# A hybrid transformer block on one core: a builder that plans every engine's order, and more seven-product quads

## The chip, the cores and the metric

The kernel runs on one core of one Trainium2 chip. The core has a matrix engine (TensorE, PE in the profile), a vector engine (VectorE, DVE), a scalar engine (ScalarE, ACT), a general engine (GpSimd, POOL) and a queue engine that issues most transfers (SyncE, SP). The metric is the device time of one execution in microseconds, the median of the runs; lower is better.

## The reference

One block of a language model, in 32-bit floats, for 256 tokens of width 2048. It is a feed-forward network, a mixer and a second feed-forward network, each between a norm before and a norm after, each added to the residual:

```python
def _swiglu(x, w_gate, w_up, w_down):                 # 2048 -> 5632 -> 2048
    return (jax.nn.silu(x @ w_gate) * (x @ w_up)) @ w_down

def _hybrid_mixer(u, ...):
    p = u @ w_in                                      # 2048 -> 3360 + 1024 + 2 * 2048
    z_a, z_b, g_a, g_b = jnp.split(p, IN_SPLITS, axis=-1)
    y_a = _rwkv7_branch(z_a, ...) @ w_proj_a          # 16 heads of 64, a recurrence over tokens
    y_b = _pool_branch(z_b, ...) @ w_proj_b           # windowed means, 4 groups
    m = jax.nn.sigmoid(g_a) * y_a + jax.nn.sigmoid(g_b) * y_b
    return m @ w_out

h = x + 0.5 * norm(_swiglu(norm(x), ffn1...))
h = h + norm(_hybrid_mixer(norm(h), ...))
out = h + 0.5 * norm(_swiglu(norm(h), ffn2...))
```

Nearly all the arithmetic is in the large products: the three weights of each feed-forward network, and `w_in`, `w_proj_a`, `w_proj_b`, `w_out` of the mixer.

## The kernel before

**A product.** A 32-bit product is made of three faster ones. Every operand is split into a high part (rounded to the fast format) and a low part (the rest): ACT writes the high part of a weight tile, `wH` (L149), DVE subtracts it from the tile and writes the low part, `wL` (L150), and `mm3` (L173 to L175) issues high x high, high x low and low x high into one PSUM bank. Tokens are the rows of the output: the activations, transposed, are the stationary operand (128 x 128), and 512 columns of a weight are the moving one. So one product of a weight row block k with one half h of the tokens is three matmuls of 128x512.

**Weights.** They come from DRAM as tiles of 128 x 1024 (two row blocks of 512 columns, 512 KB), issued by SP into four raw buffers `w32` (`get_w`, L135). Five buffers each of `wH` and `wL` follow. SP issues in order and waits for a free raw buffer.

**Quads.** Where two row blocks k, k+1, two column blocks (called f and l) and two token halves meet, eight products are needed. `seven` makes them with seven: it forms sums and differences of the weight tiles (`t13` at L344, `t24` at L349 and L350), splits them (L356 on ACT, L357 on DVE), multiplies them with sums of the activation tiles that were prepared once (`sums`), and puts the results together with adds on DVE from PSUM (`merge` at L381, `finish` at L391). One such step is called a quad here. `FAST = range(2, 10)` makes two quads in each of the eight inner blocks of gate and up, `NQ = 6` makes six in each of the two column pairs of the down product: 16 + 12 for each feed-forward network.

**A feed-forward network.** Gate and up are walked in 11 blocks of 512 columns. For a block, the f columns are those of the gate weight, the l columns those of the up weight. Then ACT makes a sigmoid and DVE multiplies (L613, L615), DVE multiplies with up (L619), and DVE turns the block in 32 x 32 squares (L545). For the down product the block's hidden units must lie on the partitions, so 16 ACT copies of 32 x 256 (L571, in `carry_at`) move the squares to the right partitions, one block later, and ACT and DVE split the result. The down product has 44 row blocks and two column pairs of 2 x 512 columns; `post` squares and sums its results for the norm, scales them and adds the residual.

**The mixer.** The products of `w_in` and of the projections fill TensorE while two halves of the heads (hf 0 and 1) go through the recurrence in chunks of 64 tokens: small matmuls (64 x 64), masks, and DVE and ACT work between them (`rwkv`). Two powers of -1/2 are made on GpSimd: the norm of the keys (L1162, 128 x 16) and the group norm of each chunk (L1386, 128 x 4).

**What sets the order.** Instructions go to each engine in program order. Large parts are ordered by hand: in the feed-forward networks, `put` gives PE work with its expected time, `at` places the ACT and DVE work at a moment of that clock, and `run` writes them out in time order; in the mixer, generators hand over PE time step by step (`weave`). Elsewhere a scheduler with priorities orders the instructions. Buffers rotate in pools.

Of the kernel before, what the change touches and what calls it, by code (L numbers as in the profile page):

```python
# [5 lines left out]

# [12 lines left out]
P = 128  # L19
# [8 lines left out]
C = 64  # L28
# [6 lines left out]
W32_BUFS = 4  # L35
WS_BUFS = 5
BOOST = 2000
MM, MC = 0.2265, 0.12
TT = 0.45
# [3 lines left out]
AHEAD = (5.0, 6.0)  # L43
TURNS = [[4.2, 5.3, 6.4, 7.5], [5.3, 6.0, 6.7, 7.4]]
WARM = 12
TB = 4
NQ = 6
QUADS = {False: ((7, 11, 15), (3, 6, 9)), True: ((2, 5, 8, 11, 14), (1,))}
FAST = range(2, 10)
# [5 lines left out]

class Block:
    def __init__(s, tc, ctx):
        s.tc = tc
        s.nc = nc = tc.nc
        E = ctx.enter_context  # L60
        s.n = 0
        s.late, s.after, s.items, s.events, s.now = [], [], deque(), [], 0.0
        s.clk, s.uses = 0.0, []
        s.cp = E(tc.tile_pool(name="cp", bufs=1))
        s.wp = E(tc.tile_pool(name="wp", bufs=3))
        s.up = E(tc.tile_pool(name="up", bufs=NUNITS))
        s.tp = E(tc.tile_pool(name="tp", bufs=TB))
        s.sp = E(tc.tile_pool(name="sp", bufs=4))
        s.dp = E(tc.tile_pool(name="dp", bufs=1, space=bass.MemoryType.DRAM))
        s.pm = E(tc.tile_pool(name="pm", bufs=4, space=PSUM))  # L70
        s.pt = E(tc.tile_pool(name="pt", bufs=4, space=PSUM))
        s.ident = s.const([P, P], "ident")
        make_identity(nc, s.ident)
        s.mhalf = s.const([P, 16], "mhalf")
        nc.gpsimd.memset(s.mhalf, -0.5)
# [4 lines left out]

    def const(s, shape, name, dt=F32):
        return s.cp.tile(list(shape), dt, tag=name, name=name)

    def unit(s, shape=(P, 1024), dt=F32, p="u"):
        return s.up.tile(list(shape), dt, tag="u", name=s.nm(p))

    def tmp(s, p="t"):
        return s.tp.tile([P, 512], F32, tag="t", name=s.nm(p))

    def rtmp(s, p="r"):  # L90
        return s.tp.tile([P, 256], F32, tag="r", name=s.nm(p), bufs=3)

    def small(s, w, tag, bufs=4):
        return s.sp.tile([P, w], F32, tag=tag, name=s.nm(tag), bufs=bufs)

    def psum(s, p="pt"):
        return s.pt.tile([P, 512], F32, tag="pt", name=s.nm(p))

    def at(s, t, fn):

        s.n += 1
        heapq.heappush(s.events, (t, s.n, fn))

    def slot(s, end):

        s.uses.append(end)
        n = len(s.uses) - 1 - WS_BUFS
        return s.uses[n] if n >= 0 else n - 1.0

    def run(s):  # L110

        s.now = 0.0
        E = mybir.EngineType
        with s.tc.manual_schedule(engines={E.PE, E.Activation, E.DVE}):
            while s.items or s.events:
                while s.events and (s.events[0][0] <= s.now or not s.items):
                    heapq.heappop(s.events)[2]()
                if s.items:
                    t, fn = s.items.popleft()
                    fn()  # L120
                    s.now += t
            s.stats()
        s.now = s.clk = 0.0
        s.uses = []

    def put(s, t, fn):
        s.items.append((t, fn))
        s.clk += t

    def get_w(s, w, j, n, c0, cw, own=False):  # L130
        if own:
            w32 = s.unit(p="w32")
        else:
            w32 = s.wp.tile([P, 1024], F32, tag="w32", name=s.nm("w32"), bufs=W32_BUFS)
        s.nc.sync.dma_start(out=w32[:, :n * cw].rearrange("p (k c) -> p k c", k=n),  # L135
                            in_=w[j * P:(j + n) * P, c0:c0 + cw]
                            .rearrange("(k p) c -> p k c", p=P))
        return w32

    def two(s, w32, j, n, cw, hold=False):  # L140
        if hold:
            wH, wL = s.unit(dt=F32R, p="kH"), s.unit(dt=F32R, p="kL")
        else:
            wH = s.wp.tile([P, 1024], F32R, tag="wH", name=s.nm("wH"), bufs=WS_BUFS)
            wL = s.wp.tile([P, 1024], F32R, tag="wL", name=s.nm("wL"), bufs=WS_BUFS)
        v, vH, vL = [t[:, :n * cw].rearrange("p (k c) -> p k c", k=n)
                     for t in (w32, wH, wL)]
        with s.tc.high_priority(offset=BOOST):
            s.nc.scalar.copy(vH, v)  # L149
            s.nc.vector.tensor_tensor(out=vL, in0=v, in1=vH.bitcast(F32), op=ALU.subtract)  # L150
        return [(j + i, vH[:, i], vL[:, i]) for i in range(n)]

# [8 lines left out]
    def split_w(s, fill):  # L161

        w32 = s.wp.tile([P, 1024], F32, tag="w32", name=s.nm("w32"), bufs=W32_BUFS)
        wH = s.wp.tile([P, 1024], F32R, tag="wH", name=s.nm("wH"), bufs=WS_BUFS)
        wL = s.wp.tile([P, 1024], F32R, tag="wL", name=s.nm("wL"), bufs=WS_BUFS)
        fill(w32.rearrange("p (a b) -> p a b", a=2))
        s.nc.scalar.copy(wH, w32)
        s.nc.vector.tensor_tensor(out=wL, in0=w32, in1=wH.bitcast(F32), op=ALU.subtract)
        return [t.rearrange("p (a b) -> p a b", a=2) for t in (wH, wL)]

    def mm3(s, ps, aH, aL, bH, bL, start, stop):
        nc = s.nc
        nc.tensor.matmul(ps, aH, bH, start=start, stop=False)  # L173
        nc.tensor.matmul(ps, aH, bL, start=False, stop=False)  # L174
        nc.tensor.matmul(ps, aL, bH, start=False, stop=stop)  # L175

    def gemm_tok(s, w, c0, at, KT, evac, lead=False, trail=False, xs=None, hold=False):
        pss = [s.pm.tile([P, 512], F32, tag="mm", name=s.nm("mm")) for _ in range(2)]
# [10 lines left out]
        def both(k0, k1):  # L189
            for k2 in range(k0, k1, 4):  # L190
                keep(s.load_w(w, k2, min(4, k1 - k2), c0, 512))
                for k in range(k2, min(k2 + 4, k1)):
# [3 lines left out]
        if trail:  # L196
            both(0, KT - TRAIL)
            s.by_half(w, c0, KT - TRAIL, KT, s.clk, AHEAD[0], do, keep,
                      lambda h: evac(h, pss[h]))
# [5 lines left out]
        elif lead:  # L205
            s.by_half(w, c0, 0, STAG, s.clk, AHEAD[1], do, keep)
            s.run()
            k0 = STAG
        both(k0, KT)
        if hold:  # L210
            for h in range(2):
                s.at(0.3 + 1.6 * h, lambda h=h: evac(h, pss[h]))
            return
        with s.tc.high_priority(offset=BOOST):
            for h in range(2):
                evac(h, pss[h])

    def gemm_at(s, w, c0, at, KT, evac):

        pss = []  # L220
        ws = {}

        def load(k):
            ws.update((i, (wH, wL)) for i, wH, wL in s.load_w(w, k, 2, c0, 512))

        def do(k):
            if not pss:
                pss.extend(s.pm.tile([P, 512], F32, tag="mm", name=s.nm("mm"))
                           for _ in range(2))
            for h in range(2):  # L230
                (wH, wL), (xH, xL) = ws[k], at(k)
                s.mm3(pss[h], xH[:, h * P:h * P + P], xL[:, h * P:h * P + P], wH, wL,
                      k == 0, k == KT - 1)
        for k in range(0, KT, 2):
            s.at(s.slot(s.clk + 12 * MM), lambda k=k: load(k))
            s.put(6 * MM, lambda k=k: do(k))
            s.put(6 * MM, lambda k=k: do(k + 1))
        for h in range(2):
            s.at(s.clk + 0.3 + 1.6 * h, lambda h=h: evac(h, pss[h]))

    def by_half(s, w, c0, k0, k1, start, ahead, do, keep, done=None):

        for k in range(k0, k1, 2):
            s.at(start + (k - k0) * 3 * MM - ahead,
                 lambda k=k: keep(s.load_w(w, k, 2, c0, 512, k - k0 >= STAG)))
        for h in range(2):
            for k in range(k0, k1):
                s.put(3 * MM, lambda k=k, h=h: do(k, h))
            if done:
                s.put(0, lambda h=h: done(h))  # L250

    def sums(s, T, out, when=None):
# [3 lines left out]
        tt = {}  # L256
        fl = lambda t: t.rearrange("p a b t -> p (a b t)")

        def first():
            xH, xL = T[len(out) // 2]  # L260
            x = tt["x"] = s.unit((P, 2, 2, S), F32, "sx")
            V.tensor_tensor(out=fl(x), in0=xH.bitcast(F32).rearrange("p k t -> p (k t)"),
                            in1=xL.bitcast(F32).rearrange("p k t -> p (k t)"), op=ALU.add)

        def second():
            x = tt["x"]
            a11, a21 = x[:, :, 0, :P], x[:, :, 0, P:]
            a12, a22 = x[:, :, 1, :P], x[:, :, 1, P:]
            f = tt["f"] = s.unit((P, 4, 2, P), F32, "sf")
            V.scalar_tensor_tensor(out=f[:, 0], in0=a21, scalar=-1.0, in1=a22, op0=ALU.mult,  # L270
                                   op1=ALU.subtract)
            V.scalar_tensor_tensor(out=f[:, 1], in0=f[:, 0], scalar=-1.0, in1=a11,
                                   op0=ALU.mult, op1=ALU.subtract)
            V.tensor_tensor(out=f[:, 2], in0=a11, in1=a21, op=ALU.subtract)
# [1244 lines left out]
```

## Time and profile before

| what | value |
|---|---|
| median of 3 runs | 2062.89 us (2062.83 to 2062.97) |
| profiled execution, span from first to last instruction | 2061.1 us |
| mean granted TensorE clock | 0.998 of full speed |
| PE / DVE / ACT / POOL busy | 2047.8 / 1638.5 / 1228.9 / 76.0 us |
| read from DRAM | 396.69 MB, 197 GB/s over the span |

The profiled execution was timed by its span alone; it lies 1.8 us below the median of the runs. A profile row names the line, the engine, the operation, `out<-in` by the tiles' names, shapes, how often it ran, busy time and the mean of one in ns, and what ended the idle time before it. `PE` is matmul, `PEld` the weight load that runs beside it. Successive matmuls overlap, so the length of one (about 0.39 us) is more than its share of the time.

### The profile page before, as it was taken

The numbers are of one execution on the slowest core, as the hardware profiler recorded it, in microseconds if no ns is written. First come the engines' busy times: TensorE is split into PE (matmuls) and PEld (weight loads), VectorE is DVE, ScalarE is ACT, GpSimd is POOL, SyncE is SP. The second block draws the span as 40 slices with busy tenths as digits, with TensorE's granted clock in tenths as the row PEclk, the third lists the DMA queues.
The fourth block names the chain that finished last, engine by engine and source line by source line (L and its number), as shares of the span: only waits on it lengthen the run. The fifth ranks groups of instructions, "written<-read, shape, count | busy, mean of one in ns | idle before, by whom it ended". The sixth has DMA issues, their size and how long they took to land.

```text
span 2061.1 us, 29467 instructions
## 1 busy us (share of the span) xinstructions
PE 2047.8 (99%) x10925; PEld 1726.6 (84%) x10925; DVE 1638.5 (79%) x2104; ACT 1228.9 (60%) x1752; POOL 76.0 (4%) x161
## 2 busy tenths in 40 slices
PE   9999999999999999999999999999999999999998
PEld 7888888888888899999888788888888888888886
DVE  6888889878787765799688666578888898787875
ACT  7667666766555574474465444466677667755553
POOL 0000000000000100000110110010000000000000
PEclk9999999999999999999999999999999999999999
DMA  7566666665667666656456565665666666656674
GB/s 259 174 195 210 195 205 194 199 220 173 215 205 254 218 188 185 179 161 199 129 158 190 163 245 187 202 215 173 194 207 195 212 194 195 220 167 218 208 251 151
DMA packets 225913, 407.02 MB, mean 197 GB/s; under 512 B 14943, under 2 KB 50921, under 8 KB 225769
## 3 DMA queue, kind: packets, MB, share of 16 engines
q1 hardware_dynamic: 219593, 384.69, 59.8%
q0 software_dynamic: 5888, 19.93, 2.7%
q8 instruction: 85, 1.39, 0.3%
q10 hardware_dynamic: 288, 0.52, 0.1%
q14 instruction: 59, 0.48, 0.1%
HBM read 396.69 MB, written 8.39 MB: 197 GB/s over the span
## 4 chain that ended last, share of the span: by engine, by line
PE 97%; issue 1%; DVE 1%; POOL 0%; DMA 0%; ACT 0%; POOLq 0%; DVEq 0%; SPq 0%; ACTq 0%
PE mm L173 26%; PE mm L175 25%; PE mm L174 25%; PE mc L500 10%; PE ms L173 2%; PE ms L175 2%; PE ms L174 2%; PE tr L528 1%; PE pA L1240 0%; PE pSa L1348 0%; PE pU L1336 0%; DMA w<-in_ffn_gate_dram 0%; DVE wL L150 0%; PE pT L1407 0%; PE pM L1306 0%
## 5 line engine op out<-in xcount | busy, mean ns | idle before, releaser
L150 DVE TENSOR_TENSOR wL<-w,wH 128x1024 fp32r<-128x1024 f32 (+2 forms) x613 | 730.3, 1207 | 274.7 <-ACT wH L149 271.2
L149 ACT CAST wH<-w 128x1024 fp32r<-128x1024 f32 (+2 forms) x613 | 631.0, 1043 | 425.9 <-PE mm L175 236.8
L173 PE MATMUL mm<-wH,xH 128*128 128x512 f32 x2124 | 830.2, 392 | 0.0
L175 PE MATMUL mm<-wH,xL 128*128 128x512 f32 x2124 | 827.2, 389 | 0.7 <-DVE xL L536 0.7
L174 PE MATMUL mm<-wL,xH 128*128 128x512 f32 x2124 | 826.9, 389 | 0.0
L175 PEld LDWEIGHTS mm<-wH,xL 128*128 128x128 f32 x2124 | 398.7, 188 | 84.8 <-DVE xL L536 1.5
L173 PEld LDWEIGHTS mm<-wH,xH 128*128 128x128 f32 x2124 | 398.6, 188 | 82.9 <-ACT xH L534 0.2
L174 PEld LDWEIGHTS mm<-wL,xH 128*128 128x128 f32 x2124 | 398.8, 188 | 81.8 <-DVE wL L150 0.3
L500 PE MATMUL mc<-xH,wH 128*128 128x256 f32 x560 | 159.5, 285 | 0.0
L500 PE MATMUL mc<-xL,wH 128*128 128x256 f32 x560 | 158.4, 283 | 0.0
L500 PE MATMUL mc<-xH,wL 128*128 128x256 f32 x560 | 158.4, 283 | 0.0
L356 ACT CAST wH<-t 128x1024 fp32r<-128x1024 f32 x112 | 117.6, 1052 | 65.4 <-PE mm L175 31.7
L356 ACT CAST wH<-w 128x1024 fp32r<-128x1024 f32 x112 | 93.9, 838 | 104.4 <-PE mm L175 45.7
L357 DVE TENSOR_TENSOR wL<-t,wH 128x1024 fp32r<-128x1024 f32 x112 | 134.2, 1219 | 24.7 <-ACT wH L356 24.5
L571 ACT COPY x<-T 32x256 f32<-32x256 f32 x352 | 142.2, 404 | 12.2 <-DVE T L545 6.3
L500 PEld LDWEIGHTS mc<-xH,wH 128*128 128x128 f32 x560 | 106.0, 189 | 1.1
L500 PEld LDWEIGHTS mc<-xH,wL 128*128 128x128 f32 x560 | 106.0, 189 | 0.2
L500 PEld LDWEIGHTS mc<-xL,wH 128*128 128x128 f32 x560 | 106.0, 189 | 0.1
L357 DVE TENSOR_TENSOR wL<-w,wH 128x1024 fp32r<-128x1024 f32 x112 | 102.2, 950 | 1.3 <-ACT wH L356 1.3
L344 DVE TENSOR_TENSOR t<-w,w 128x1024 f32<-128x1024 f32 x56 | 68.2, 1219 | 22.3 <-DMA w<-in_ffn_down_dram 20.8
L173 PE MATMUL ms<-wH,sH 128*128 128x512 f32 x168 | 65.4, 389 | 0.0
L175 PE MATMUL ms<-wH,sL 128*128 128x512 f32 x168 | 65.4, 389 | 0.0
(297 smaller groups left out, 1864.0 us busy)
## 6 DMA issues: line engine op xcount, KB each, us to landing
w<-in_ffn_up_dram SPq DMA_DIRECT2D x144, 512.0 KB
w<-in_ffn_gate_dram SPq DMA_DIRECT2D x142, 512.0 KB
w<-in_ffn_down_dram SPq DMA_DIRECT2D x128, 512.0 KB
w<-in_w_in_dram SPq DMA_DIRECT2D x128, 512.0 KB
w<-in_ffn_down_dram SPq DMA_DIRECT2D x96, 256.0 KB
w<-in_ffn_gate_dram SPq DMA_DIRECT2D x68, 256.0 KB
w<-in_ffn_up_dram SPq DMA_DIRECT2D x64, 256.0 KB
w<-in_w_out_dram SPq DMA_DIRECT2D x32, 512.0 KB
```

Source lines behind the costliest of these rows:

```text
L149: s.nc.scalar.copy(vH, v)
L150: s.nc.vector.tensor_tensor(out=vL, in0=v, in1=vH.bitcast(F32), op=ALU.subtract)
L173: nc.tensor.matmul(ps, aH, bH, start=start, stop=False)
L174: nc.tensor.matmul(ps, aH, bL, start=False, stop=False)
L175: nc.tensor.matmul(ps, aL, bH, start=False, stop=stop)
L344: V.tensor_tensor(out=v["t13"], in0=v["a"], in1=v["b0"].to_broadcast([P, 2, 512]), op=ALU.subtract)
L356: nc.scalar.copy(H, v[n_])
L357: V.tensor_tensor(out=L, in0=v[n_], in1=H.bitcast(F32), op=ALU.subtract)
L500: s.nc.tensor.matmul(o, lh, rh, start=one and n == 0, stop=k == KT - 1 and n == 2, skip_group_check=True)
L528: nc.tensor.transpose(ps[:, i], src[:, i * P:(i + 1) * P], s.ident)
L571: nc.scalar.copy(dst[q * 32:q * 32 + 32, :, :, i], src[i * 32:i * 32 + 32, :, :, q])
```

## The change

The kernel is written anew around a planner; the mathematics is the same but for the quads.

**A plan of all engines.** Every call to an engine is recorded (`Plan.add`) with its reads and writes and a cost. `deadlines` works back from the order of the matmuls to the time by which each instruction should be done, `simulate` runs the five engines by those costs and takes on each the ready instruction with the earliest deadline (on PE: the recurrence's `chain` first, then `side` transposes, then `main`), assigns each tile to a slot of its pool when it starts, and `emit` writes all instructions out in that order, with a dependency on whoever used the slot before:

```diff
+            slow = name == "matmul" and r[0].dtype == F32
+            o.pace = 2 * (0.7 * c + 32) / 2.4 if slow else (c + 32) / 2.4
+            o.dur = o.pace + 165
+        elif o.eng == "ACT":
+            ...
+            o.pace, o.dur = n / 1.2 + 103 + extra, n / 1.2 + 200 + extra
+        elif o.eng == "DVE":
+            ...
+            o.pace, o.dur = n * f + 75 + more, n * f + 158 + more
+        else:
+            o.pace = o.dur = n * 1.0 + 110
...
+                if x.stream == "chain" and x.eng == "PE" and e != "PE":
+                    t += 250
...
+        with s.tc.manual_schedule():
+            for o in order:
+                ins = o.fn(*[real(x) for x in o.a], **{n: real(x) for n, x in o.k.items()})
+                ...
+                    for b in before:
+                        s.tc.add_manual_dep(ins.ins, b.ins.name, info, reason="slot")
```

(`n` are the elements of a partition, `c` the columns of a matmul, times are in ns.) `put`, `at`, `run`, the generators of the mixer and the priorities are gone.

**Sizes.**

```diff
-W32_BUFS = 4
+W32_BUFS = 5
-TB = 4
-NQ = 6
-FAST = range(2, 10)
+TB = 6
+AHEAD = 25000.0
+EASE = 2.0
+GATE_QUADS = [0, 0] + [3] * 7 + [2, 2]
+DOWN_QUADS = ((8, 1, 2.4), (8, 1, 1.7))
+SCRATCH = 1024
```

`TB` counts the temporary tiles of 128 x 512. Quads are now 25 + 16 for each feed-forward network.

**Gate and up.** A quad of gate and up is cut in two. `early` (four products) runs while the block before is under way, into the four PSUM banks of the next block, which alternate between the two pools; `join` then puts the four results together inside PSUM, and everything that follows, `late` (three products) included, accumulates on top:

```diff
+    def join(s):
+        q, b = s.b, s.banks
+        A, V = q.nc.scalar, q.nc.vector
+        u0, s2, p5 = [q.tmp(n) for n in ("u0", "s2", "p5")]
+        A.copy(u0, b["l0"])
+        A.copy(p5, b["f0"])
+        V.tensor_tensor(out=b["f1"], in0=b["f1"], in1=u0, op=ALU.add)
+        A.copy(s2, b["f1"])
+        V.tensor_tensor(out=b["f0"], in0=b["f0"], in1=s2, op=ALU.add)
+        V.tensor_tensor(out=b["l1"], in0=b["l1"], in1=s2, op=ALU.add)
+        V.tensor_tensor(out=b["f1"], in0=b["l1"], in1=p5, op=ALU.add)
```

The quads of the down product keep separate banks and a `merge` as before.

**Silu and the carry.** Gate's result goes through one ACT pass with the Silu function instead of a sigmoid on ACT and a multiply on DVE. The 16 ACT copies of a block's carry are 16 transfers from SBUF to SBUF on SP's queue:

```diff
-        for i in range(4):
-            for q in range(4):
-                nc.scalar.copy(dst[q * 32:q * 32 + 32, :, :, i],
-                               src[i * 32:i * 32 + 32, :, :, q])
+    def carry(s, T1, T):
+        x = s.unit((P, 1024), F32, "x32")
+        for i in range(4):
+            for q in range(4):
+                nc.sync.dma_start(out=x[q * 32:q * 32 + 32, i * 256:i * 256 + 256],
+                                  in_=T1[i * 32:i * 32 + 32, q * 256:q * 256 + 256])
```

with the turn on DVE writing its squares in the order that these transfers read, and two splits (one for each token half) behind them.

More of the change, by code (lines that the diff above doesn't have):

```diff
@@ L53, with __init__, __getattr__ @@
 ROWS2 = [("r_k", 8), ("gn_w", 8), ("gn_b", 8), ("pool_scale", 8)]
+class Op:
+    __slots__ = ("eng", "fn", "a", "k", "pace", "dur", "preds", "succs", "dl", "nom",
+                 "stream", "tiles", "new", "left", "ready", "start", "end", "i", "tab",
+                 "nbytes", "lag")
+class TileInfo:
+    __slots__ = ("tag", "left", "slot", "seq", "writes", "reads", "psum", "dl", "home")
+class Engine:
+    def __init__(s, plan, key, real):
+        s.plan, s.key, s.real = plan, key, real
+    def __getattr__(s, name):
+        fn = getattr(s.real, name)
+        return lambda *a, **k: s.plan.add(s.key, name, fn, a, k)
@@ L99, in at @@
[L99 to L124, printed above, removed]
@@ L205, in gemm_tok @@
         elif lead:
-            s.by_half(w, c0, 0, STAG, s.clk, AHEAD[1], do, keep)
-            s.run()
+            s.by_half(w, c0, 0, STAG, do, keep)
             k0 = STAG
         both(k0, KT)
[L210 to L237, printed above, removed]
@@ L487, in ch_g @@
[L487 to L505 removed]
+        ps = s.psum("warm")
@@ new lines, in head @@
+        for _ in range(WARM):
+            s.nc.tensor.transpose(ps[:, :P], s.ident, s.ident)
+        load(0, 0)
+        load(1, 0)
+        load(None, None)
+        for k in range(4):
+            get(k, 1)
+        for c in range(1, 4):
+            load(0, c)
+            get(4 * c, 2)
+            load(1, c)
+            get(4 * c + 2, 2)
+        split(0)
+        turn(0, 0)
+        split(1)
+        turn(1, 0)
+        split(2)
+        split(3)
+        for k in range(KT):
+            do(k, 0)
+            do(k, 1)
+            if k % 2 == 0 and k + 4 < KT:
+                turn(k // 2 % 2, k // 4 + 1)
+                split(k + 4)
@@ new lines, with block_seq @@
+class Kernel(Block):
+    def block_seq(s, J, N, ev):
+        own = []
+        nf = len(J.rest)
+        lates = list(J.quads)
+        for i, k in enumerate(J.rest):
+            own.append(lambda k=k: J.pair(k, "f"))
+            while lates and (i >= 1 or i == nf - 2):
+                k2 = lates.pop(0)
+                own.append(lambda k=k2: J.late(k))
+                if i < nf - 2:
+                    break
+        own.append(lambda: ev("f"))
+        for k in J.rest:
+            own.append(lambda k=k: J.pair(k, "l"))
+        if N and N.quads:
+            n, m = len(N.quads), len(own)
+            pos = [round((i + 0.5) / n * (m - 3)) for i in range(n)]
+            for i in reversed(range(n)):
+                items = [lambda k=N.quads[i]: N.early(k)]
+                if i == n - 1:
+                    items.append(N.join)
+                own[pos[i]:pos[i]] = items
+        for fn in own:
+            fn()
+        ev("l")
@@ new lines, in evac, with hold @@
+            return ev
+        ev = evac(rs, [], None)
+        pss = [], []
+        def hold(i):
+            return lambda h, ps: (pss[i].append(ps), h and ev("fl"[i], pss[i]))
+        s.gemm_tok(wg, 0, at, NKD, hold(0), lead=True, xs=xs)
+        s.gemm_tok(wu, 0, at, NKD, hold(1))
+        while s.after:
+            s.after.pop(0)()
+        rb = s.rtmp("rsb")
+        s.spread(rs, rb)
+        su = []
+        nT = s.normed(uT, rb, su)
+        jobs = {}
+        for b in range(1, nb):
+            jobs[b] = Columns(s, wg, b * 512, wu, b * 512, s.T_at(nT) if b > 1 else at, NKD,
+                              su, [2 * i for i in range(GATE_QUADS[b])],
+                              s.psum if b % 2 else s.bank)
@@ L665, in spread @@
+        for b in range(1, nb):
+            J = jobs[b]
+            s.block_seq(J, jobs.get(b + 1), evac([1.0, 1.0] if b > 1 else rs, [], J.banks))
+        s.down(wd, s.T_at(hT), gpost, resid, emit, reload, hT, sm)
     def spread(s, rs, out):
@@ L691, in one @@
                             op=ALU.mult)
-            s.at(s.now + 1.5, lambda: nc.scalar.copy(fl(nH), fl(x)))
-            s.at(s.now + 4, last)
-        for i in range(len(uT)):
-            s.at(t + 9.5 * i, lambda i=i: one(i))
-        return nT
-    def post(s, wd, at, KT, gpost, fac, resid, emit, reload, hT=None, sm=None):
+            s.split(fl(x), fl(nH), fl(nL))
+            if i < (max(GATE_QUADS) + 1) // 2:
+                s.sums(x.rearrange("p (a b) t -> p a b t", a=2), su)
+        return nT
@@ L751, in post, with norm @@
[L751 to L760 removed]
+        def norm(h, r):
+            r2 = s.small(1, "rt2", bufs=2)
+            nc.vector.tensor_scalar(out=r2, in0=ss[h][:, 3:4], scalar1=kf,
+                                    scalar2=part[h], op0=ALU.mult, op1=ALU.add)
+            nc.gpsimd.tensor_tensor(out=r, in0=r2, in1=s.mhalf[:, :1], op=ALU.pow)
```

1273 lines of the change are left out of this document (728 added, 545 removed).

## The prediction

> **What bounds the kernel now.** I read the page's totals and slices first, then the chain that ended last, then the busy time by stretches, then single rows.
>
> ```profile
> span 2061.1 us, 29467 instructions
> PE 2047.8 (99%) x10925; PEld 1726.6 (84%) x10925; DVE 1638.5 (79%) x2104; ACT 1228.9 (60%) x1752; POOL 76.0 (4%) x161
> PE   9999999999999999999999999999999999999998
> PEclk9999999999999999999999999999999999999999
> PE 97%; issue 1%; DVE 1%; POOL 0%; DMA 0%; ACT 0%; POOLq 0%; DVEq 0%; SPq 0%; ACTq 0%
> ```
>
> TensorE is busy in every slice, its clock is granted in full, and it is 97% of the chain that ended last. So the kernel is as long as its list of matmuls: a change is worth the matmuls it drops, less whatever it makes TensorE wait. A busy share can hide a PE that runs below its pace, so I need the pace of one matmul. The last rows of the span give it, and show what follows the last matmul:
>
> ```profile
> 2049.23 0.39 PE L175 MATMUL mm<-kH,xL 128*128 128x512 f32 x1
> ...
> 2051.27 0.39 PE L175 MATMUL mm<-kH,xL 128*128 128x512 f32 x1
> 2051.69 0.69 DVE L391 TENSOR_TENSOR u<-mm,u 128x512 f32<-128x512 f32 x1 [5.39 <-PE mm L175]
> 2054.48 2.74 DVE L747 SCALAR_TENSOR_TENSOR fg<-fg,rs,h 128x512 f32<-128x512 f32 x4 [0.44 <-POOL rs L743]
> ```
>
> Nine steps from 2049.23 to 2051.27 are 0.2267 us each; the 0.39 of a row is its own length, overlapped by the next. The end after it, some 10 us of adds, scaling and output, is built the same way afterwards, so I leave it alone. Now the stretches (columns: PE, PEld, DVE, ACT, POOL busy, each with its count; clock, DMA share, GB/s):
>
> ```profile
> 100.00:438.00 338.00, 338.00 (x1493) 279.89 (x1492) 299.72 (x328) 232.59 (x321) 0.00 (x0) 1.00 0.63 201
> 144.70:186.80 42.10, 42.10 (x188) 34.85 (x187) 37.43 (x41) 28.90 (x41) 0.00 (x0) 1.00 0.62 199
> 480.00:718.00 238.00, 238.00 (x1060) 197.05 (x1059) 191.13 (x216) 131.45 (x166) 6.75 (x12) 1.00 0.67 214
> 718.00:1017.00 299.00, 298.39 (x2490) 282.42 (x2489) 225.03 (x401) 165.69 (x270) 22.46 (x52) 1.00 0.61 177
> 1017.00:1373.00 356.00, 355.43 (x2272) 291.50 (x2271) 252.67 (x412) 186.62 (x290) 37.55 (x54) 1.00 0.59 187
> ```
>
> In the gate/up blocks of FFN1 (100 to 438), 1493 matmuls take 338.00 us: 0.2264 each, no gap at all. The second row is one block of 42.1 us with two quads, the third the down product. VectorE is the nearest rival there, 89% and 80% busy. The last two rows are the mixer; summing over its matmuls what each start lies behind the pace of its shape, I find about 14 us of waiting, and next to none in the FFNs. So an FFN's time can come only from fewer matmuls, and the mixer has a little to win back.
>
> **Part 1, more quads: the gain.** A quad saves one of eight products, three 128x512 matmuls. GATE_QUADS is 25 per FFN where FAST had 16; down has 8 per column pair where NQ was 6, so 16 for 12. That is 13 more per FFN, 26 in all, 78 matmuls: 78 x 0.2267 = **-17.7 us**. The built program has just these 78 fewer.
>
> **Its price on VectorE and ScalarE.** These groups have it:
>
> ```profile
> L357 DVE TENSOR_TENSOR wL<-t,wH 128x1024 fp32r<-128x1024 f32 x112 | 134.2, 1219 | 24.7 <-ACT wH L356 24.5
> L357 DVE TENSOR_TENSOR wL<-w,wH 128x1024 fp32r<-128x1024 f32 x112 | 102.2, 950 | 1.3 <-ACT wH L356 1.3
> L344 DVE TENSOR_TENSOR t<-w,w 128x1024 f32<-128x1024 f32 x56 | 68.2, 1219 | 22.3 <-DMA w<-in_ffn_down_dram 20.8 <-issue 0.7 <-DMA w<-in_ffn_gate_dram 0.6
> L350 DVE TENSOR_TENSOR t<-w,t 128x512 f32<-128x512 f32 x56 | 38.7, 692 | 2.3 <-DMA w<-in_ffn_down_dram 0.5
> L349 DVE TENSOR_TENSOR t<-w,t 128x512 f32<-128x512 f32 x56 | 38.7, 692 | 1.9
> L381 DVE TENSOR_TENSOR u<-ms,u 128x512 f32<-128x512 f32 x80 | 53.2, 686 | 1.4
> L615 DVE TENSOR_TENSOR u<-u,ms 128x512 f32<-128x512 f32 x32 | 20.4, 680 | 0.0
> L571 ACT COPY x<-T 32x256 f32<-32x256 f32 x352 | 142.2, 404 | 12.2 <-DVE T L545 6.3
> ```
>
> A quad costs DVE (134.2 + 102.2 + 68.2 + 38.7 + 38.7) / 56 = 6.82 us; the two plain weight tiles that it replaces cost 2 x 1.219 = 2.44; so one more quad adds 4.38. The join in PSUM has four adds where merge and finish had eight, -4 x 0.686 = -2.74. Silu in one ACT pass takes the two multiplies of L615 away, -1.36. A block with three quads then keeps DVE busy for 37.43 + 4.38 - 2.74 - 1.36 = 37.7 us, beside a PE time of 42.1 - 3 x 0.2267 = 41.4: 91%, with 3.7 us to spare. In the down product, four more quads and one more group of sums (under 5 us) give 191.1 + 17.5 + 4 = 213 of 235 us, again 91%. So DVE stays below PE in the mean, and I cost its extra work at **nothing**, with the weight tiles split ahead (five buffers of 12 matmuls, 5 x 2.72 = 13.6 us) as the cover. One place is dearer. At the start of FFN1's block 1, `normed`, its sums, the first turn and the weight splits stand together in the built order: 25 DVE rows between the end of `wu` and the first tile for the new block, about 17.5 us by their mean durations, against 17.7 us of matmuls ready. From 0 to +2 us; I take **+1**.
>
> ScalarE loses the 16 carry copies of a block, 352 x 0.404 = 142 us in all, and is 60% busy before that. Nothing comes of it on the path.
>
> **Part 2, the carry by DMA.** Sixteen small DMAs (32 KB, SBUF to SBUF) go into SP's queue for each of 22 blocks. Every weight tile behind them waits, first for the turn on DVE that they wait for and then for their issue. These rows bound one issue:
>
> ```profile
> 22.17 0.27 SPq L802 DMA_DIRECT2D cols<-in_rwkv_w_dram  x1
> 23.51 0.27 SPq L802 DMA_DIRECT2D cols<-in_rwkv_a_dram  x1
> ...
> 27.22 0.29 SPq L802 DMA_DIRECT2D cols<-in_rwkv_gn_w_dram  x1
> 27.56 0.29 SPq L802 DMA_DIRECT2D cols<-in_rwkv_gn_b_dram  x1
> SPq L135 <- DVE wL L150: 903.7, 434, 12.7
> ```
>
> Free-running, 27.22 to 27.56, they are 0.34 us apart: 16 x 0.34 = 5.4 us. Where each had to wait for an earlier one, 22.17 to 23.51, 1.34 apart: 21.4 us. The last row says that SP mostly waits for a free weight buffer (434 times), so all buffers are normally full. The cover is five raw tiles, 13.6 us, and as much again already split, 27.2. Both ends lie under 27.2, the likelier one well under 13.6. I take **0**; the other end is a rival below.
> The Trainium skill speaks against this part: "DMA: Bandwidth & Descriptors", section "Measured", says that transfers under 64 KB are descriptor-dominated, and its "Anatomy of one DMA" gives each a fixed cost of about 2 us. Taken in series, my estimate by that page is 32 us per block, 4.8 beyond the 27.2 of cover, 22 x 4.8 = 106 us in all: 2157. The rows 0.34 us apart show small DMAs that overlap; no carry by DMA is in this trace.
>
> **Part 3, the planned order.** The plan gives the mixer's chain priority on PE. Each visit to a 64-row group and back costs time, as here:
>
> ```profile
> 1178.85 0.39 PE L175 MATMUL mm<-wH,xL 128*128 128x512 f32 x1
> 1179.17 0.68 PE L1348 MATMUL pSa<-us,R 64*64 64x64 f32 x16
> 1179.78 0.50 PE L173 MATMUL mm<-wH,xH 128*128 128x512 f32 x1
> 1180.12 0.39 PE L174 MATMUL mm<-wL,xH 128*128 128x512 f32 x1
> ```
>
> From 1178.85 to the group is 0.32 where a matmul takes 0.227, and the matmul after it takes 0.34 before the next starts: 0.09 + 0.11 = 0.20 us per visit, the group's own time apart. The built order has 107 runs of such groups between main matmuls, before had 82. I count 15 of the 25 more as visits of this kind, 15 x 0.2 = **+3**; between 0 and 25 x 0.2 = 5.
>
> The plan decides which DVE row goes where by costs of its own. DVE, ACT and matmul costs in it agree with the rows above. Its cost of a GpSimd op, elements + 110 ns, doesn't:
>
> ```profile
> L1386 POOL TENSOR_TENSOR g<-g,mhalf 128x4 f32<-128x4 f32 x8 | 8.1, 1018 | 43.9 <-DVE g L1383 43.9
> L1162 POOL TENSOR_TENSOR n<-n,mhalf 128x16 f32<-128x16 f32 x2 | 6.7, 3373 | 46.9 <-DVE fx L1049 27.9 <-DVE n L1160 19.1
> 886.20 0.16 DVE L1160 TENSOR_SCALAR n<-pn 128x16 f32<-128x16 f32 x1
> 890.83 0.69 DVE L1164 COPY R<-n 128x1024 f32<-128x1024 f32 x1
> ```
>
> These are the two powers of the mixer, 3.37 us for the norm of kk and 1.02 for each chunk's group norm, planned at 0.13 and 0.11. Before, DVE has 4.6 us of other rows between writing n and reading its power (886.20 to 890.83). In the new order only three short scans stand between them, then DVE waits, and behind it on DVE stand the scans, the pool sums and the weight splits, for which PE waits in turn. The kk power is 3.24 us short, twice: 0 to +6.5; the first half's stands ahead of a stretch in which DVE's rows add up to slightly more than PE's, the second has slack. I take **+2**. The chunk power is 0.9 short, eight times: 0 to +7.2; DVE waits then, but PE feels it only where a chain group comes next. **+2**.
>
> Against that, the order now favours the chain, and of the mixer's 14 us of waiting some should go: between -6 and 0, I take **-2**, as the rows that wait there wait for one another and not for a free engine.
>
> **The sum.** 2061.1 - 17.7 + 1 + 0 + 3 + 2 + 2 - 2 = 2049.4 for the profiled span. The median of the runs is 2062.9, 1.8 above the span, so **2051.2** by the median. All costs at their low end give 2061.1 - 17.7 - 6 + 1.8 = 2039.2, all at the high end (2 + 5 + 6.5 + 7.2 = 20.7) give 2065.9.
>
> **Rivals.**
> The order is nearly free (the costs together 3 us or less): 2045 less what the chain gives back, 2039 to 2046. For it: the FFNs run at pace, and half of my costs are bounds on the mixer alone. Chance 0.12.
> The mixer eats the gain: the two powers and the visits at their upper ends and the win-back absent, 2059 to 2067, no change that a measurement can tell (0.2% is 4.1 us: 2058.8 to 2067.0). For it: the plan is wrong by a factor of 10 to 25 on these ops, and an order fixed by hand can't move around a late one. Against: 24% and more of DVE's time in the mixer is free, so a wait is caught up. Chance 0.07. That the matmuls are not gone would land here too; the built program excludes it but for 0.01.
> The carry holds the weight stream (slower): if the carries go out at intervals of i, SP is away for 16 i, and past the raw lead of 13.6 us splits run dry. The point is i = 0.85; at 0.92 each block loses 16 x 0.92 - 13.6 = 1.1 us, 22 x 1.1 = 24 us, 2075; at 1.34 it is 7.8 x 22 = 172 us, 2223, if the split tiles cover nothing. For it: the queue's own rows at 1.34. Against: the rows at 0.34, and 27.2 us of cover with the split tiles counted. The page's series of 2 us belongs here. Chance 0.05.
> VectorE becomes the bound (slower): three-quad blocks would have to need over 41.4 us. From 37.7, it decides at 10% more than the rows say; at 44 us, 14 blocks lose 2.6 each, 36 us, 2087. For it: 91% leaves little for uneven stretches. Against: 89% costs nothing today. Chance 0.03.
>
> **The numbers.** The forecast itself (2046 to 2058.8) has 0.72, the free order 0.12: faster 0.84. No change 0.08, slower 0.08. The likeliest time is 2051.2. The range 2041 to 2061 leaves out some of the lower rival, most of the mixer's worst case and both slower ones, under 0.2 together.
>
> **What would show it.** Right: 128x512 matmuls fewer by 78; the FFN stretches still at 0.2267 a matmul, each FFN some 8.8 us shorter; the mixer longer than before by 3 to 6 us, with DVE waiting for POOL where the powers are. Wrong: SP's carry rows over 0.85 us apart, with splits waiting for weight DMAs once per block; PE waiting for wL in the three-quad blocks; or a mixer that is shorter than before, which would refute the costs of part 3.

## The result, and the profile after

The changed kernel takes 2152.11 us (2148.96 to 2155.24), the kernel before 2062.93 us: 89 us slower, a ratio of 1.0432 (95% interval 1.0417 to 1.0446). The forecast was 2051.2 and its range ended at 2061. Its profiled execution has a span of 2153.5 us. First, from the page of the changed kernel: its totals, two lines of its slices, the line on DRAM and the chain that ended last:

```profile
span 2153.5 us, 30194 instructions
PE 2076.4 (96%) x10847; PEld 1724.4 (80%) x10847; DVE 1669.6 (78%) x2176; ACT 1141.9 (53%) x1520; POOL 74.8 (3%) x146
PE   9899999999999999999999999999999999999998
PEclk9999999999999999999999999999999999999999
HBM read 422.91 MB, written 8.39 MB: 200 GB/s over the span
PE 47%; DVE 18%; issue 12%; SPq 11%; DMA 8%; ACT 3%; POOL 0%; DVEq 0%; ACTq 0%; POOLq 0%
```

The digits of the slices hide it: they still show nines. The chain does not: PE was 97% of it and is 47%, and SP's queue and transfers, which had no share, have 19%. The line on DRAM holds the second surprise, 422.9 MB read where before read 396.7. The gate/up blocks of the two FFNs have the largest part of the loss, about half in each. This is the same stretch of FFN1 as in the prediction, for the changed kernel, and below it for the same kernel with the carry on another queue (the experiment `carry_pool`):

```profile
100.00:438.00 338.00, 318.93 (x1354) 255.65 (x1353) 272.66 (x303) 177.34 (x213) 0.00 (x0) 0.98 0.70 229
```

```profile
100.00:438.00 338.00, 338.00 (x1493) 279.88 (x1492) 296.77 (x326) 195.70 (x231) 62.60 (x128) 1.00 0.78 252
```

1354 matmuls in 338 us where 1493 fit: 139 x 0.2267 = 31.5 us lost in this stretch alone. With the carry elsewhere, the 1493 are there again, and DVE is busy for 88% of the stretch (the forecast was 91%).

From the start times of all matmuls I split each span into matmuls at pace, what 128x512 and 128x256 matmuls wait beyond it, the time of all other groups on PE, and the ends. A matmul that starts late because the clock is lower counts as waiting here. The third column has the carry on GpSimd's queue; the last has, besides, the true cost of the powers in the plan (`pool_pow` below):

| us | before | after | carry on GpSimd | and powers booked right |
|---|---|---|---|---|
| 128x512 at 0.2267 | 1746.3 | 1728.6 | 1728.6 | 1728.6 |
| 128x256 at 0.12 | 207.4 | 207.4 | 207.4 | 207.4 |
| wait at 128x512 | 14.3 | 113.5 | 34.2 | 25.4 |
| wait at 128x256 | 1.9 | 6.7 | 6.7 | 9.0 |
| other PE groups | 79.7 | 86.7 | 86.9 | 84.8 |
| ends | 11.6 | 10.6 | 10.6 | 10.6 |
| span | 2061.2 | 2153.5 | 2074.4 | 2065.8 |

The 17.7 us of matmuls are gone, as counted. Of the 99 us more waiting at 128x512, the gate/up blocks of both FFNs have 67, the first 80 us have 7, the down products 12, the two passages between an FFN and the mixer 6, the mixer itself 7.

**What happens in a block.** One carry, on SP's queue, in the changed kernel:

```profile
212.63 0.43 SPq L391 DMA_DIRECT2D w<-in_ffn_up_dram  x1
213.18 10.01 SPq L391 DMA_DIRECT2D x<-T  x16
223.29 0.53 SPq L391 DMA_DIRECT2D w<-in_ffn_gate_dram  x1
223.86 0.43 SPq L391 DMA_DIRECT2D w<-in_ffn_up_dram  x1
224.39 0.38 SPq L391 DMA_DIRECT2D w<-in_ffn_gate_dram  x1
```

Sixteen transfers take 10.0 us to issue, one every 0.633 us, and for that long no weight is asked for. It is so in all 22 blocks: no weight transfer stands between the first and the last of a carry. The same place by stretches, then on ACT, then on PE:

```profile
200.00:213.00 13.00, 13.00 (x59) 10.76 (x58) 13.00 (x17) 5.93 (x6) 0.00 (x0) 1.00 0.80 265
213.20:225.00 11.80, 11.80 (x53) 9.77 (x53) 7.74 (x8) 5.06 (x6) 0.00 (x0) 1.00 0.34 96
225.00:235.00 10.00, 8.62 (x36) 6.25 (x35) 6.30 (x8) 2.81 (x4) 0.00 (x0) 1.00 0.91 319
```

```profile
224.57 1.14 ACT L391 CAST xH<-x 128x512 fp32r<-128x512 f32 x2 [3.79 <-DMA x<-T]
226.94 1.05 ACT L391 CAST wH<-w 128x1024 fp32r<-128x1024 f32 x1 [1.23 <-DMA w<-in_ffn_up_dram]
230.67 1.05 ACT L391 CAST wH<-w 128x1024 fp32r<-128x1024 f32 x1 [2.68 <-DMA w<-in_ffn_gate_dram]
235.28 1.05 ACT L391 CAST wH<-w 128x1024 fp32r<-128x1024 f32 x1 [3.56 <-PE f L391]
```

```profile
231.77 0.50 PE L391 MATMUL f<-wH,xH 128*128 128x512 f32 x1 [0.35 <-ACT wH L391]
233.03 0.50 PE L391 MATMUL f<-wL,xH 128*128 128x512 f32 x1 [0.76 <-DVE wL L391]
...
236.38 0.49 PE L391 MATMUL l<-wH,xH 128*128 128x512 f32 x1 [0.56 <-ACT wH L391]
237.64 0.50 PE L391 MATMUL l<-wL,xH 128*128 128x512 f32 x1 [0.77 <-DVE wL L391]
```

The last number of the stretches is GB/s: 265 ahead of the carry, 96 during it, 319 after it, with the DMA engines 91% busy. PE keeps its pace through the hole (53 matmuls in 11.8 us) on what was split ahead, and pays 6 to 15 us after its end. At 231.77 and 233.03 a weight tile goes from landing to cast to subtraction to matmul with nothing in hand, and PE waits for ACT and then for DVE. The pair at 236.38 and 237.64 is of another kind: its cast stood 3.56 us waiting for PE to release a buffer of split weights. Such pairs are the exception. I followed each delay of 0.1 us or more in the gate/up blocks of both FFNs, 65 us in all, back through ACT and DVE to the wait that ended last: 47 us end at the landing of a weight, 5 at a split buffer that PE still held, and 13 are matmuls just behind a wait that start late without one of their own (0.34 us after the first, and 0.427 us apart where the clock was lowered). The unexpected 26 MB are the reread: `late` fetches row k+1 of both weights again, which `early` had already read, 100 transfers of 256 KB. With them a block asks for about 250 GB/s (the 252 above) where before asked for 200, so a hole empties the tiles sooner, and the 319 at which they fill again leaves less over.

### The profile page after: what moved, and what is told of

Read it like the earlier page. It is cut to its first block, busy times and chain, and to the rows that moved or that the text cites. A ratio compares the mean times of both kernels' runs of the same rounds, so it can differ in the third digit from the quotient of the medians.

```text
span 2153.5 us, 30194 instructions
## 1 busy us (share of the span) xinstructions
PE 2076.4 (96%) x10847; PEld 1724.4 (80%) x10847; DVE 1669.6 (78%) x2176; ACT 1141.9 (53%) x1520; POOL 74.8 (3%) x146
## 4 chain that ended last, share of the span: by engine, by line
PE 47%; DVE 18%; issue 12%; SPq 11%; DMA 8%; ACT 3%; POOL 0%; DVEq 0%; ACTq 0%; POOLq 0%
PE l L391 14%; SPq L391 11%; PE f L391 9%; PE mm L391 9%; DVE wL L391 9%; PE mc L391 8%; DMA w<-in_ffn_gate_dram 5%; PE p L391 3%; ACT wH L391 2%; DVE t L391 2%; DVE w L391 1%; DVE sg L391 1%; DMA w<-in_ffn_up_dram 1%; DMA w<-in_ffn_down_dram 1%; DVE pr L391 1%
## 5 line engine op out<-in xcount | busy, mean ns | idle before, releaser
L391 PE MATMUL l<-wL,xH 128*128 128x512 f32 x772 | 303.9, 394 | 12.2 <-DVE wL L391 12.2
L391 PE MATMUL l<-wH,xH 128*128 128x512 f32 x772 | 303.3, 393 | 10.8 <-ACT wH L391 10.8
L391 PE MATMUL l<-wH,xL 128*128 128x512 f32 x772 | 301.7, 391 | 0.0
L391 PE MATMUL f<-wL,xH 128*128 128x512 f32 x664 | 261.2, 393 | 14.8 <-DVE wL L391 14.8
L391 PE MATMUL f<-wH,xH 128*128 128x512 f32 x664 | 260.1, 392 | 1.3 <-ACT wH L391 1.3
L391 PE MATMUL f<-wH,xL 128*128 128x512 f32 x664 | 259.7, 391 | 0.0
L391 PE MATMUL mm<-wL,xH 128*128 128x512 f32 x500 | 198.7, 397 | 3.0 <-DVE wL L391 3.0
L391 PE MATMUL mm<-wH,xH 128*128 128x512 f32 x500 | 197.3, 395 | 0.0
L391 PE MATMUL mm<-wH,xL 128*128 128x512 f32 x500 | 197.2, 394 | 0.0
L391 PEld LDWEIGHTS mm<-wL,xH 128*128 128x128 f32 x500 | 94.5, 189 | 23.8 <-DVE wL L391 4.3
```

The source lines that it names most:

```text
L391: ins = o.fn(*[real(x) for x in o.a], **{n: real(x) for n, x in o.k.items()})
```

## The experiments

The theories, as lettered in the expectations: A, the unbroken hole of 10 us in SP's queue starves PE; B, the reread and the third quad have eaten the lead; C, the transfers themselves slow the weights; D, the plan's wrong cost for them misplaces them; E, DVE is too full to catch up. The changed kernel is 2152.1, before 2063.0 in all of these. Where an edit changes the engine or the cost of an instruction, the plan is made anew, so other rows move too.

**The carry by ACT copies.**

```diff
-                nc.sync.dma_start(out=x[...], in_=T1[...])
+                nc.scalar.copy(x[...], T1[...])
```

> The changed kernel with the 16 transfers of each carry replaced by 16 ACT copies of 32x256 (as before the change); the plan is made anew with them. Theory A (SP's queue issues nothing else for 16 x 0.633 = 10.1 us, so the weight stream has a hole and PE runs dry behind each carry, about 4 us x 20 blocks): 2065 to 2080. Theory B (the extra quads, with their third raw tile and the second read of row k+1, have eaten the lead of the weight stream; the carry only shows it): over 2115.

Measured: 2083.5 us (2082.9 to 2085.1). The wait of the gate/up blocks falls from 67 to 7 us. As A says, with 3.5 us more than its range; theory B, as I wrote it there (over 2115), is out.

**The carry on GpSimd's queue.** `nc.gpsimd.dma_start` for `nc.sync.dma_start`.

> The changed kernel with the same 16 transfers issued by GpSimd instead of SP. Theory A: SP is free for weights, so 2065 to 2090, the upper end if GpSimd's own issue makes the carry land late. Theory C (it is not the issue but the transfers themselves, which share the 16 DMA engines with the weights and delay them): no better than 2140.

Measured: 2075.8 us (2075.1 to 2076.1); the gate/up blocks wait 1.0 us. The same bytes between the same places cost the blocks next to nothing: C is out. They land later there, and the blocks don't wait for it. The medians from issue to landing, on SP and on GpSimd:

```profile
x<-T SPq DMA_DIRECT2D x352, 32.0 KB, 1.8
```

```profile
x<-T POOLq DMA_DIRECT2D x352, 32.0 KB, 3.4
```

**The plan told the true cost.**

```diff
             o.pace = {"SP": 370.0, "ACT": 110.0, "POOL": 600.0}[o.eng]
+            if o.nbytes == 32768 and o.eng == "SP":
+                o.pace = 633.0
```

> The changed kernel, but the plan books 633 ns for each carry transfer on SP, as measured, where it booked 370; nothing else is altered. If the wrong cost is what hurts (theory D: the plan would have spread the transfers, or put weights ahead of them): below 2090. If the hole itself hurts, however well it is known (theory A): 2125 to 2152.

Measured: 2153.1 us (2150.2 to 2156.2), no change, 1 us past the upper end that A gave. The plan still issues the 16 in a row, 10.0 us long; D is out.

**The carry alone, in the kernel before.** `carry_at` issues 16 `nc.sync.dma_start` in place of the copies; with them come the turn's new layout and a split in two halves, as in the changed kernel.

> The kernel before with the change's carry alone: 16 transfers per block on SP's queue, the turn's layout that they need and a split in two halves, in place of the 16 ACT copies. All else as before: two quads, four raw tiles. Theory A: a hole of 10.1 us against four raw tiles of 2.72 us, 10.9 us less the landing of the next weight: 1 to 4 us for most of 22 blocks, 2080 to 2150. Theory B: the lead of this kernel is whole, so 2060 to 2066.

Measured: 2069.0 us (2068.1 to 2070.4), a ratio of 1.0029 (1.0018 to 1.0039). So the carry costs 6 us there and 76 in the changed kernel: less than A by itself said (2080 or more), more than B (2066 at most). Its SP rows show two differences:

```profile
277.20 6.61 SPq L571 DMA_DIRECT2D x<-T  x9
283.92 0.52 SPq L135 DMA_DIRECT2D w<-in_ffn_up_dram  x1
284.48 0.51 SPq L571 DMA_DIRECT2D x<-T  x1
285.40 0.34 SPq L339 DMA_DIRECT2D w<-in_ffn_up_dram  x1
285.86 0.83 SPq L339 DMA_DIRECT2D w<-in_ffn_gate_dram  x2
286.74 0.43 SPq L339 DMA_DIRECT2D w<-in_ffn_up_dram  x1
287.21 3.68 SPq L571 DMA_DIRECT2D x<-T  x6
```

The scheduler of that kernel happened to let five weights go between the ninth and the last six, and its demand is 200 GB/s. Four or five weights stand inside the carry in 18 of its 22 blocks. How much of the 70 us each of the two differences is worth, this run alone doesn't say.

**No reread.** `late` splits a tile that is already in SBUF and fetches nothing, so the second reading of row k+1 is left out and the numbers of another tile are multiplied in its place.

> The changed kernel, carry on SP as it is, but `late` reads nothing: it splits and multiplies a resident tile in place of the two transfers of 256 KB that fetch row k+1 again, so 100 transfers, 26 MB and a raw tile per gate quad are left out; all instructions of PE, ACT and DVE stay. Theory A alone (the 10 us hole of SP empties the five tiles whatever the demand): 2135 to 2150. Theory B together with A (the reread lifts the demand from 200 to about 250 GB/s, so that the tiles last shorter and are refilled at 320 GB/s too slowly): the loss behind the carries falls from about 4 us a block to 1 or less, 2075 to 2095.

Measured: 2119.8 us (2116.5 to 2123.9), between the two ranges: 32 of the 89 us go. The blocks wait 38 us instead of 67. The reread makes the hole worse by three quarters; it isn't the whole of it. At 200 GB/s, as in the kernel before, a carry in one piece still costs 38 us of waiting here.

**Two quads for three.**

> The changed kernel with two quads in every gate/up block instead of three (GATE_QUADS), carry on SP: 14 quads fewer, 42 matmuls more, +9.5 us on PE; a third of the reread gone, DVE some 4 us per block freer. Theory A/B by demand: 226 GB/s instead of 249, the loss per block falls from 4 to about 2.5 us, 2125 to 2140. Theory E (DVE at 90% can't catch up after a hole): with DVE at 80% the loss falls under 1 us per block, 2085 to 2105.

Measured: 2137.1 us (2131.7 to 2138.8). The blocks wait 44 us, as theory A/B with its lower demand had it (2125 to 2140). E, which gave 2105 at most, is out: DVE four us freer per block doesn't fill the hole.

**The carry spread on SP.** Same transfers, same queue; in the plan SP takes a weight first whenever one can go:

```diff
+                    if e == "SP":
+                        big = [x for x in av if ops[x[1]].nbytes != 32768
+                               and can(ops[x[1]])]
+                        if big:
+                            av.remove(min(big))
+                            heapq.heapify(av)
+                            go(ops[min(big)[1]])
+                            moved = True
+                            continue
```

> The changed kernel with the same 16 carry transfers still on SP (633 ns booked for each), but the plan lets SP issue a weight transfer first whenever one can go, so that the carry goes out in groups of 1 to 6 between weights instead of 16 in a row; no transfer is added or left out. If the unbroken hole of 10 us is what empties the raw tiles (theory A): 2070 to 2095, with next to no loss behind the carries. If the time SP spends issuing, or the carry's bytes, cost wherever they stand (theory C): 2130 to 2153.

Measured: 2080.1 us (2078.6 to 2081.2): 73 us less than with the true cost and no spreading (2153.1). In most blocks the carry now takes 15 to 17 us instead of 10, in pieces, and PE doesn't wait behind it:

```profile
198.42 1.78 SPq L402 DMA_DIRECT2D x<-T  x3
200.30 0.53 SPq L402 DMA_DIRECT2D w<-in_ffn_gate_dram  x1
200.87 0.43 SPq L402 DMA_DIRECT2D w<-in_ffn_up_dram  x1
201.34 2.42 SPq L402 DMA_DIRECT2D x<-T  x4
203.86 0.53 SPq L402 DMA_DIRECT2D w<-in_ffn_gate_dram  x1
204.43 1.14 SPq L402 DMA_DIRECT2D x<-T  x2
```

Together with `carry_cost` and `carry_pool` this settles A: not the bytes, nor the issue time as such, but that it stands in one piece ahead of the weights.

**The powers, with the carry on GpSimd.**

```diff
             o.pace = o.dur = n * 1.0 + 110
+            if k.get("op") == ALU.pow:
+                o.pace = o.dur = {1: 950.0, 4: 1020.0, 16: 3370.0}[n]
```

> The changed kernel with the carry on GpSimd (2075.8 us) and the plan's cost of a power on GpSimd set to what the trace has (0.95, 1.02 and 3.37 us for 1, 4 and 16 elements, where the plan booked elements + 110 ns). If the powers, placed as if they took 0.1 us, make the mixer's extra 17 us: 2060 to 2066. If other misplacements make it: 2072 to 2077.

Measured: 2066.3 us (2064.3 to 2071.3), 9.5 less, at the edge of what the first theory gave (2066); 1.0014 (1.0005 to 1.0024) of before. DVE's waits for these two powers, in the kernel before, in the changed one, and here (us, times, longest):

```profile
DVE R L1387 <- POOL g L1386: 1.2, 1, 1.2
DVE R L1164 <- POOL n L1162: 0.2, 1, 0.2
```

```profile
DVE yn L391 <- POOL g L391: 6.1, 6, 1.2
DVE nb L391 <- POOL n L391: 5.2, 2, 2.6
```

```profile
DVE yn L393 <- POOL g L393: 2.6, 3, 1.2
```

The wait for the norm of the keys (`n`) is no longer there, and that for the group norm (`g`) is less than half: the plan finds other rows for DVE once it knows how long a power takes.

**Both on SP.** The spread kernel with the powers booked right.

> The kernel with the carry spread on SP and the powers booked at 0.95, 1.02 and 3.37 us. By theory A and the gain of 9.5 us that the powers brought with the carry on GpSimd: 2062 to 2085, that is the spread kernel less 8 to 11. If the powers' gain hung on the carry's queue: as the spread kernel.

Measured: 2069.5 us (2067.4 to 2073.7), 10.7 less than spread, where the powers brought 9.5 with the carry on GpSimd: the two effects add.

The next three build on the kernel with the carry on GpSimd and the powers booked right (2066.3).

**Two quads in block 2 alone**, to free DVE at the start of each FFN.

> Carry on GpSimd, powers booked as measured, and two quads instead of three in block 2, whose early products are prepared during block 1 together with the normalized activations: +1.4 us of matmuls, DVE freed by 4.4 us in each block 1. If that place is tight as the stall of 2.1 us at 69.7 says: 2062 to 2065 (3 to 5 us less loss at the start of FFN1, nothing in FFN2). If the stall comes from the transposes' order alone: 2067 to 2068.

Measured: 2069.2 us (2067.5 to 2070.4), 2.9 more than without, and outside both ranges. The first 80 us do wait 2.4 us less, but 1 us comes back in the blocks, 1.4 in matmuls, and the mixer, planned anew behind it, waits 2.4 more. A miss.

**Later quads in the second column pair of the down product.**

```diff
-DOWN_QUADS = ((8, 1, 2.4), (8, 1, 1.7))
+DOWN_QUADS = ((8, 1, 2.4), (8, 3, 1.5))
```

The plan also books 0.62 us for the copies of 64x256 on GpSimd.

> Carry on GpSimd, powers booked as measured (2066.3 us), the copies of 64x256 on GpSimd booked at 0.62 us, and in the second column pair of the down product the first quad after three plain pairs instead of one and then every 1.5 pairs. If the two waits of that place (0.8 and 1.1 us, and a slower clock behind them, in each network) come from DVE having the adds of the first pair, the scaling and a quad's preparation at once: 3 to 5 us less, 2061 to 2064. If DVE is too full there for any spacing: 2066 or more.

Measured: 2066.7 us (2063.8 to 2068.0). The down products' waits (2.2 and 3.7 us) are gone, as meant, and the mixer waits some 4 us more, though nothing was changed there but the cost of 16 copies. No gain. The time is the one of the second theory (DVE too full for any spacing), but not for its reason: the spacing did remove the waits.

**More room for chain results.** 500 for 250 ns, beside the kernel of `down_late` (2066.7).

> The same, and the plan allows 500 instead of 250 ns between a result on DVE or ACT and a matmul of the recurrence that needs it. If the 4.6 us in which PE waits at the start of a chain group (pM, pB, pT) come from the plan being too early there: 2 to 4 us less than the kernel beside it. If they come from DVE rows that stand in front: no difference beyond 1 us, or a loss.

Measured: 2067.5 us (2066.1 to 2069.0), no difference beyond 1 us: those waits aren't from too small a margin. What makes the last 5 us at chain groups is open. No version beat the kernel before.

## Why the prediction was wrong, point by point

**Part 2, the carry, "I take 0": the step that failed.** It is 76 of the 89 us (2152.1 to 2075.8). Three things in it were off. The issue: I priced it by rows of other small transfers, 0.34 us free-running, and it is 0.633, so 10 us instead of 5.4. That alone would have left my 0 standing, since 10 is under the 13.6 us of raw tiles. The cover is what failed: I took 13.6 us of raw tiles and as much split as if a full store could be drawn down and filled again for nothing. A hole is made good at 319 less 250 GB/s at most, the first weight behind it lands only some 4 us after its issue (medians 4.2 to 4.7 for the gate and up weights), and PE still waits 15 us after the carry's end. And the demand: I priced a quad on PE, DVE and ACT and overlooked that `late` reads 512 KB again, which is in the code and would have been seen by adding up the bytes of a block. At 250 GB/s my estimate of the five raw tiles is 5 x 524 KB / 250 = 10.5 us instead of 13.6, hardly more than the hole, before that landing is counted. `no_reread` gives 32 us for the rereading.

The rival "the carry holds the weight stream" named the mechanism, and what to look for, and had 0.05. Its point, i = 0.85, was set by a raw lead of 13.6 us; with 10.5 it would lie at 0.66, and with the landing behind the hole 0.633 was past it. In the kernel before, with its pieces and its lower demand, the carry cost 6 us in all. The Trainium skill's rule that I weighed ("DMA: Bandwidth & Descriptors", "Measured", and its fixed cost of about 2 us in "Anatomy of one DMA") spoke against the change. That section of the Trainium skill gives the fixed cost for transfers on GpSimd's path. Here they land after 1.8 us on SP and 3.4 on GpSimd. That my estimate by it, 2157, lies 5 us from the measured time is luck: it took the 16 in series, and they are issued 0.633 us apart and overlap; what hurt was the issue. On that the Trainium skill ("DMA: Bandwidth & Descriptors", "Issuing engines are not separate DMA queues") holds that another issuing engine saves only sequencer time, usually small; here the sequencer's time was the cost, and another engine saved 76 us.

**Part 1, the quads: right in the gain and in the gate/up blocks.** 78 matmuls fewer at an unchanged 0.2267 us. DVE in the blocks: 297 of 338 us, 88%, with no gap on PE once the carry is away; I said 91%. Block 1: said +1 (0 to 2); the waits of the first 80 us grew by 2.1 with the carry on GpSimd, by 7.3 with it on SP. In the down products the extra quads were not free, as I had it: PE waits 4 us there with the carry out of the way, and `down_late`, which places them later, takes these waits away.

**Part 3.** Visits: said +3, measured 3.5 (67 visits and 10.3 us of switching in the mixer before, 92 and 13.8 after). That is luck in part: 25 visits more where I counted 15, at 0.14 us each where I took 0.20. Powers: the mechanism was right, the size was 9.5 where I took 4, inside the bounds. The win-back of 2 did not come and had little to come from: of the 14 us that I called waiting in the mixer before, 10.3 are those switches. Not foreseen at all: 6 us at the two passages between an FFN and the mixer, of which the powers' right cost brings back some 4.

**The sum without the carry** would have been 2075.8 where I said 2051.2: even so outside the range and on the other side of before. Of the 25 us between, by the same split, the mixer has 12 (it cost 17 where my terms had 5), the passages 6, the down products 4, the start 3 (4 us longer in all, with the groups that aren't 128x512). The powers explain 5.5 of the mixer's and the passages' 18; the rest is waits that the planned order puts there, and no single cause of them is shown.

## What to carry to other kernels

When transfers move to a queue that also feeds weights, price the queue: issue time times count, in one piece or in pieces, against the lead, and the bytes that a stage asks for against the rate at which a hole can be filled. Spreading the same transfers, or giving them to another engine's queue, is worth trying before giving them up. An order planned from a cost table can lose by one wrong entry: that of the powers cost 9.5 us here, that of the carry nothing. Compare each entry with a row of the trace, the rare operations too, and expect that any change to it moves waits of some microseconds elsewhere.

## What the runs showed of the hardware that I had not expected

Sixteen SBUF-to-SBUF transfers of 32 partitions x 1 KB stand 0.633 us apart on SP, the weight transfers of 256 and 512 KB behind them in the rows above 0.52 (four steps from 223.29 to 225.37): the issue doesn't follow the bytes.

An idle time of 1.97 us was followed by a lower clock of TensorE. In the kernel with the powers booked right, matmuls around 70 us, and the stretch from 69.70 with its granted clock of 0.73:

```profile
69.73 0.39 PE L393 MATMUL f<-wH,xH 128*128 128x512 f32 x1
72.09 0.50 PE L393 MATMUL f<-wL,xH 128*128 128x512 f32 x1 [1.97 <-DVE wL L393]
...
73.24 0.63 PE L393 MATMUL f<-wL,xH 128*128 128x512 f32 x1
73.66 0.63 PE L393 MATMUL f<-wH,xL 128*128 128x512 f32 x1
```

```profile
69.70:76.00 6.30, 4.33 (x12) 3.13 (x11) 6.30 (x8) 1.44 (x3) 0.15 (x1) 0.73 0.46 140
```

They start 0.427 us apart for 3 us, so the wait of 2.1 beyond pace costs another 1.7 (nine steps from 72.09 to 75.80 take 3.71 us, at pace 2.04). The length of the idle time alone doesn't decide. With the carry on GpSimd and the powers' old cost, PE waits the same 1.97 us at the same place, and the clock stays at 1.00, with 20 matmuls in the stretch instead of 12:

```profile
71.70 0.50 PE L391 MATMUL f<-wL,xH 128*128 128x512 f32 x1 [1.97 <-DVE wL L391]
```

```profile
69.70:76.00 6.30, 4.33 (x20) 3.58 (x20) 6.02 (x7) 1.14 (x2) 0.00 (x0) 1.00 0.47 144
```

In the kernel with the powers booked right, two waits of 0.63 and 0.87 us that end at 1943.83 and 1945.21 are followed, a microsecond later, by matmuls 0.427 us apart again. So one run can lose 1.7 us at a wait that costs another nothing more. The Trainium skill ("TensorE: Matmul & The Clock Gate", Part 1) puts the drop behind an idle window of about 3.4 us; here shorter idle times were followed by it, and the rows decide. What else decides is not shown.
